# An encoder's first-layer values as seven quarter products ahead of the heads

## The chip, the cores and the metric

One core of a Trainium2 chip runs the whole program. The metric is the device time of one execution in microseconds (us): the median of 3 runs before the change is 657.52 us. Engines are named as the profile names them: PE (TensorE, with PEld for its weight loads), DVE (VectorE), ACT (ScalarE), POOL (GpSimd) and SP (SyncE, which issues most DMAs).

## The reference, cut to what matters

A two-layer encoder over 512 tokens of width 1024. Layer 0 mixes tokens by neighbourhood attention, layer 1 by multi-head latent attention; each mixer's output is gated by SiLU(z), projected and added, and a gated per-layer embedding follows. The change is in layer 0's input projection, in the third of its four parts:

```python
def mixer_na(xn, w_in, rpb, w_out):
    B, S, _ = xn.shape
    hd = NA_HEADS * NA_HEAD_DIM
    q, k, v, z = jnp.split(xn @ w_in, 4, axis=-1)
    shp = (B, S, NA_HEADS, NA_HEAD_DIM)
    o = neighbourhood_attention(q.reshape(shp), k.reshape(shp), v.reshape(shp), rpb)
    return (o.reshape(B, S, hd) * jax.nn.silu(z)) @ w_out
```

`v` is a 512 x 1024 matrix: 512 normalised tokens times 1024 x 1024 weights, used by 16 heads of 64 columns.

## The kernel before, in words

**Arithmetic.** Every float32 factor of a product is kept as two float32r tiles: `hi`, a rounded copy that ACT writes, and `lo`, the remainder `x - hi`, which DVE or POOL writes. A product is then three: hi x hi, lo x hi and hi x lo. So a block of 128 tokens, 512 output columns and a depth of 1024 costs 3 x 8 = 24 matmuls of 512 columns. `load_w` (L72) loads a weight tile of 128 x 1024 into `wraw`, has ACT write `whi` (L83) and POOL `wlo` (L84); there are three slots of each ("wp" pool), so a new tile waits for the matmuls of the third one before it.

**Order.** The program is written in one order, and a scheduler makes the order on each engine from it: of the instructions that are ready it takes the one that stands first in the program. `issue_after` pins an instruction behind another one.

**Stages around the change.** The first stage ("pre" pool, L971) loads the transposed input into `xs` (eight tiles of 128 x 512), computes the embedding product of layer 0 (`ple`, its outputs stored to DRAM at L480), the row norms, and the gates z for head pairs 0 and 1; then it scales `xs` in place to the normalised input (L1019, DVE) and splits it into `xT`, hi on ACT (L1020) and lo on DVE and POOL in turn (L1021). Gates z for pairs 2 to 4 follow (L1022, multiplied at L176).

Then `na_heads` (L224) runs. `values()` (L230) makes the first 512 columns of v: four blocks of tokens in four PSUM banks, the weights in four tiles `na_v0` of 256 rows by 512 columns (the names in the profile leave the number out: `na_v`), 96 matmuls at L238, and evacuates them into tiles `vt` by `v_split` (L215). The two other quarters of v are made inside the loop over head pairs, when `project(4)` and `project(6)` start (L247 to L260): each loads two tiles `na_v1` and runs 4 x 24 matmuls of 256 columns (through `mms`, L107). `project(j)` otherwise makes the queries and keys of head pair j (48 matmuls of 512 columns), and `attend(j)` the two heads: scores (L351, L352), softmax, transposes (L386, L388), and the product with the values (L400). `project(j + 1)` stands ahead of `attend(j)` in the program. In `attend(0)` to `attend(7)` one sum for the seven-product gates is issued per head (`sum_step`, L518: POOL issues DMAs of 1 MB that add in DRAM).

**The seven-product form** is in the kernel already, for the gate of each layer (`gate_seven`, L567): a product of two 2 x 2 block matrices from seven block products instead of eight, with the sums of weight blocks made in DRAM by DMAs beforehand (`quarters`, `sum_step`), the mixes of the left factor made by DVE out of PSUM (`keep_half`), and the combining of results in PSUM banks. Its matmuls are at L643, and all its subtractions for weights run on POOL, in halves of 512 columns (L588).

Of the kernel before, what the change touches and what calls it, by code (L numbers as in the profile page):

```python
# [40 lines left out]
class Trunk:  # L41
# [182 lines left out]
    def na_heads(self, pool, xT, zs, oT):  # L224
        nc, a = self.nc, self.a
        xh, xl = xT
        X = lambda t, k, kt: t[k // 4][:, k % 4, kt * P:(kt + 1) * P]
        V, A, U = {}, {}, {}

        def values():  # L230

            pss = [self.psum(b) for b in ("T", "T", "T", "O")]
            for c in range(4):
                w = self.load_w(a["na_v0"][c], 1024)
                for i, (s, r) in enumerate(((0, 0), (1, 0), (0, 1))):
                    for kt, ps in enumerate(pss):
                        for k in (2 * c, 2 * c + 1):
                            nc.tensor.matmul(ps, X((xh, xl)[s], k, kt), w[r][:, k % 2 * S:(k % 2 + 1) * S],  # L238
                                             start=k == 0 and i == 0, stop=k == KD - 1 and i == 2)
            for g in range(2):  # L240
                V[g] = [pool.tile([P, S], F32R, name="vt", tag="vt", bufs=8) for kt in range(NT)]
            for kt, ps in enumerate(pss):
                for g in range(2):
                    self.v_split(V[g][kt], ps[:, g * 256:(g + 1) * 256])

        def project(j):
            if j in (4, 6):  # L247
                g = j // 2
                wv = [self.load_w(a["na_v1"][g - 2, c], 1024) for c in range(2)]
                vts = V[g] = []  # L250
                for kt in range(4):
                    ps = self.psum("mm")
                    W = lambda s, k: wv[k // 4][s][:, (k % 4) * 256:(k % 4 + 1) * 256]
                    t = [(X(xh, k, kt), W(0, k)) for k in range(KD)]
                    t += [(X(xl, k, kt), W(0, k)) for k in range(KD)]
                    t += [(X(xh, k, kt), W(1, k)) for k in range(KD)]
                    self.mms(ps[:, :256], t)
                    vt = pool.tile([P, S], F32R, name="vt", tag="vt", bufs=8)
                    self.v_split(vt, ps[:, :256])
                    vts.append(vt)  # L260
# [53 lines left out]
        values()  # L314
# [648 lines left out]
    def run(self):  # L963
# [7 lines left out]
        with tc.tile_pool(name="pre", bufs=4, reuse_waits="tile") as pool:  # L971
# [10 lines left out]
            xs = [pool.tile([P, S], F32, name="xT", tag="xT", bufs=8) for k in range(KD)]  # L982
# [18 lines left out]
            xt = [pool.tile([P, D], F32, name="x", tag="x", bufs=4) for t in range(NT)]  # L1001
# [5 lines left out]
            self.ple(pool, 0, "pe", 6, operands)  # L1007
# [15 lines left out]
        oT = ([self.bigtile(f"oh{g}") for g in range(2)], [self.bigtile(f"ol{g}") for g in range(2)])  # L1023
        with tc.tile_pool(name="na", bufs=2, reuse_waits="tile") as pool:
            last = self.na_heads(pool, xT, zs, oT)
# [143 lines left out]
def layouts(i):  # L1169
# [4 lines left out]
    f = {}  # L1174
# [9 lines left out]
    def tiles(w, n):  # L1184
        k, m = w.shape
        return w.reshape(k // P, P, m // n, n).transpose(2, 1, 0, 3)
# [4 lines left out]
    f["na_v1"] = c(tiles(w[:, 2560:3072], 256).reshape(2, P, 2, 1024).transpose(0, 2, 1, 3))  # L1191

    def rows(w):
        return c(tiles(w, S).reshape(2, P, 4, 1024).transpose(0, 2, 1, 3))

    f["na_v0"] = c(tiles(w[:, 2048:2560], S).reshape(P, 4, 1024).transpose(1, 0, 2))
# [63 lines left out]
```

## Time and profile before

| what | value |
| --- | --- |
| time, 3 runs | 657.03, 657.52 (median), 657.75 us |
| span of the profiled execution, first to last instruction | 655.8 us (its time outside the span isn't given) |
| mean granted PE clock in the span | 0.997 |
| PE busy | 646.2 us, 3419 matmuls |
| DVE, ACT, POOL busy | 398.1, 441.2, 433.8 us |
| read from and written to HBM | 89.99 and 25.17 MB |
| `values()` on PE | 44.92 to 66.68 us of the span |

How to read it: a row of the groups gives line, engine and operation, the tile written `<-` the tiles read, the shape and the count, then busy time and the mean of one in ns, then the engine's idle time ahead of them and what ended it. A row of a line's own view gives the shortest, median and longest duration in ns, and the first and last start. A row of the timeline gives start, length of a merged piece, engine and line. A row of the chain gives start, length, and what the end of the program was waiting on at that time. Durations of matmuls overlap, since they are pipelined; their pitch, from a piece of the chain divided by its count, is what they cost.

### The profile page before, as it was taken

The numbers are of one execution on the slowest core, as the hardware profiler recorded it, in microseconds if no ns is written. First come the engines' busy times: TensorE is split into PE (matmuls) and PEld (weight loads), VectorE is DVE, ScalarE is ACT, GpSimd is POOL, SyncE is SP. The second block draws the span as 40 slices with busy tenths as digits, with TensorE's granted clock in tenths as the row PEclk, the third lists the DMA queues.
The fourth block names the chain that finished last, engine by engine and source line by source line (L and its number), as shares of the span: only waits on it lengthen the run. The fifth ranks groups of instructions, "written<-read, shape, count | busy, mean of one in ns | idle before, by whom it ended". The sixth has DMA issues, their size and how long they took to land.

```text
span 655.8 us, 10132 instructions
## 1 busy us (share of the span) xinstructions
PE 646.2 (99%) x3419; PEld 551.6 (84%) x3419; DVE 398.1 (61%) x854; ACT 441.2 (67%) x879; POOL 433.8 (66%) x383
## 2 busy tenths in 40 slices
PE   9999999999999999999999999999999999999994
PEld 6888888998988888888899888888888888888884
DVE  6190355845646526569825613888888886464665
ACT  7672587766767743687743635897979897537855
POOL 0496475895685664697764626785969887436974
PEclk9999999999999999999999999999999999999998
DMA  9944254996675889435743334120111223673524
GB/s 329 348 134 140 96 197 134 249 233 143 215 161 184 199 171 373 169 129 157 252 120 114 103 98 148 51 76 5 64 55 65 65 71 123 226 287 129 191 67 160
DMA packets 44756, 102.18 MB, mean 156 GB/s; under 512 B 4640, under 2 KB 17696, under 8 KB 44704
## 3 DMA queue, kind: packets, MB, share of 16 engines
q1 hardware_dynamic: 33776, 83.97, 38.1%
q0 software_dynamic: 10496, 16.78, 11.8%
q10 hardware_dynamic: 432, 0.79, 0.3%
q8 instruction: 27, 0.44, 0.3%
q14 instruction: 25, 0.20, 0.1%
HBM read 89.99 MB, written 25.17 MB: 176 GB/s over the span
## 4 chain that ended last, share of the span: by engine, by line
PE 98%; ACT 0%; DVE 0%; issue 0%; POOLq 0%; POOL 0%
PE ps_mm L107 35%; PE ps_S L107 12%; PE ps_mm L751 7%; PE ps_T L139 6%; PE ps_T L643 5%; PE ps_O L863 5%; PE ps_mm L643 3%; PE ps_S L643 3%; PE ps_T L107 3%; PE ps_T L238 2%; PE ps_O L400 2%; PE ps_O L107 2%; PE ps_mm L701 2%; PE ps_mm L184 2%; PE ps_T L388 2%; PE ps_S L701 1%
## 5 line engine op out<-in xcount | busy, mean ns | idle before, releaser
L84 POOL TENSOR_TENSOR wwlo<-wraw,wwhi 128x1024 fp32r<-128x1024 f32 (+5 forms) x78 | 143.2, 1852 | 76.4 <-ACT wwhi L83 54.7
L83 ACT ACTIVATE wwhi<-wraw 128x1024 fp32r<-128x1024 f32 (+5 forms) x81 | 65.5, 832 | 61.1 <-issue 19.2
L588 POOL TENSOR_TENSOR wlo<-wraw,whi 128x512 fp32r<-128x512 f32 x56 | 73.6, 1346 | 25.2 <-ACT whi L586 19.0
L848 POOL TENSOR_TENSOR ex<-ex,rc 128x512 f32<-128x512 f32 x64 | 66.3, 1045 | 25.8 <-DVE rc L847 22.0
L846 ACT ACTIVATE ex<-ps_S,mx 128x512 f32<-128x512 f32 x64 | 44.0, 688 | 11.7 <-DVE mx L844 10.1
L844 DVE TENSOR_REDUCE mx<-ps_S 128x1 f32<-128x512 f32 x64 | 43.7, 682 | 8.3 <-PE ps_S L107 7.7
L96 DVE TENSOR_TENSOR pt_lo<-ps_T,pt_hi 128x512 fp32r<-128x512 f32 x64 | 43.1, 681 | 7.1 <-ACT pt_hi L94 6.7
L374 POOL TENSOR_TENSOR ex<-ex,rc 128x128 f32<-128x128 f32 (+1 forms) x64 | 36.1, 621 | 15.0 <-DVE rc L370 15.0
L107 PE MATMUL ps_mm<-xh,wwhi 128*128 128x512 f32 x152 | 40.3, 398 | 0.0
L94 ACT ACTIVATE pt_hi<-ps_T 128x512 fp32r<-128x512 f32 x64 | 37.8, 595 | 3.4 <-PE ps_T L139 3.0
L107 PE MATMUL ps_mm<-xl,wwhi 128*128 128x512 f32 x152 | 38.5, 391 | 0.0
L139 PE MATMUL ps_T<-ident,ex 128*128 128x128 f32 x256 | 38.3, 272 | 0.0
L107 PE MATMUL ps_mm<-xh,wwlo 128*128 128x512 f32 x152 | 38.2, 391 | 0.0
L139 PEld LDWEIGHTS ps_T<-ident,ex 128*128 128x128 f32 x256 | 31.5, 140 | 7.5
L107 PEld LDWEIGHTS ps_mm<-xh,wwlo 128*128 128x128 f32 x152 | 28.3, 188 | 6.0
L586 ACT ACTIVATE whi<-wraw 128x1024 fp32r<-128x1024 f32 x28 | 29.2, 1055 | 5.9 <-DMA wraw<-sum 3.0
L107 PEld LDWEIGHTS ps_mm<-xl,wwhi 128*128 128x128 f32 x152 | 28.3, 188 | 5.7
L205 DVE TENSOR_TENSOR u<-ps_O,u 64x512 f32<-64x512 f32 x32 | 22.0, 686 | 17.2 <-ACT u L204 16.7
L368 ACT ACTIVATE ex<-ex,mx 128x128 f32<-128x128 f32 (+1 forms) x64 | 30.3, 475 | 2.7 <-DVE mx L358 1.8
L107 PEld LDWEIGHTS ps_mm<-xh,wwhi 128*128 128x128 f32 x152 | 27.3, 188 | 4.8
L209 POOL TENSOR_TENSOR u<-u,z 128x512 f32<-128x512 f32 x16 | 21.9, 1371 | 13.6 <-DVE u L205 8.3
L107 PE MATMUL ps_S<-ko,qo 128*128 128x512 f32 x96 | 28.9, 409 | 0.0
(441 smaller groups left out, 1849.8 us busy)
## 6 DMA issues: line engine op xcount, KB each, us to landing
sum<-gate POOLq DMA_DIRECT2D x12, 1024.0 KB, 7.8
wraw<-na_qk SPq DMA_DIRECT2D x16, 512.0 KB, 3.4
wraw<-sum SPq DMA_DIRECT2D x16, 512.0 KB, 3.3
pe<-pe SPq DMA_DIRECT2D x31, 256.0 KB, 6.9
wraw<-gate SPq DMA_DIRECT2D x12, 512.0 KB, 3.3
wraw<-na_v SPq DMA_DIRECT2D x8, 512.0 KB, 4.1
sum<-sum POOLq DMA_DIRECT2D x4, 1024.0 KB, 10.9
wraw<-na_o SPq DMA_DIRECT2D x8, 512.0 KB, 5.4
```

The costliest lines, as they stand in the source:

```text
L83: nc.scalar.activation(hi[:, c], raw[:, c], AF.Copy)
L84: f = lambda e, c=c: e.tensor_tensor(out=lo[:, c], in0=raw[:, c], in1=hi[:, c].bitcast(F32), op=ALU.subtract)
L94: self.last_copy = nc.scalar.activation(hi, src, AF.Copy, scale=scale)
L96: nc.vector.tensor_tensor(out=lo, in0=src, in1=hi.bitcast(F32), op=ALU.subtract)
L107: last = self.last_mm = nc.tensor.matmul(out, l, r, start=i == 0, stop=i == n - 1)
L139: self.last_mm = self.nc.tensor.transpose(t[:, i * P:(i + 1) * P], b, self.ident)
L588: nc.gpsimd.tensor_tensor(out=lo[:, o], in0=raw[:, o], in1=hi[:, o].bitcast(F32), op=ALU.subtract)
L643: mm = nc.tensor.matmul(ps, l, r, start=j == 0 and p in banks, stop=j == 11 and p in (2, 3, 4), skip_group_check=True)
L751: self.last_mm = nc.tensor.matmul(PS[key], *terms[i], start=i == 0, stop=i == len(terms) - 1)
L844: nc.vector.reduce_max(mx, sp, axis=AX.X, negate=True)
L846: nc.scalar.activation(ex, sp, AF.Exp, bias=mx, accum_out=sm)
L848: nc.gpsimd.tensor_tensor(out=ex, in0=ex, in1=rc.to_broadcast([P, S]), op=ALU.mult)
```

## The change

- The values of all 16 heads are made ahead of the loop over heads, by a new function `values_seven`; `values()` and the value parts of `project(4)` and `project(6)` are gone. Tokens are halved, the depth is halved and the columns are halved; the seven products have 256 tokens (two blocks i of 128), a depth of 512 and 512 columns. Each takes 12 matmuls of 512 columns per block i. They run in the order 1, 2, 7, 6, 4, 5, 3, each matmul pinned behind the one before it.
- The mixes of x for products 7, 5, 6 and 3 are made by POOL in place in `xs` (now two tiles `xk` of four), each 128 x 1024; ACT writes their hi part and DVE their lo part, into four of the big tiles `V7`, `V5`, `V6`, `V3`, which take the slots of `raw`, the unscaled x of the z gates.
- The weights come as eight tiles of 128 x 1024 (`R`), loaded at the start of the stage's own pool. Four products use sums or differences of two quarters: DVE makes these in place, one tile of 1024 columns after another. ACT writes the hi part of each of the 14 tiles; DVE writes the lo part of the first tile of each product, POOL that of the second, in halves of 512 columns. The tiles are in the three slots of the "wp" pool and two pairs of their own ("vw").
- Results are combined in PSUM: product 2 is accumulated on 1, 4 on 7, 5 and 3 on 6, with copies by ACT and sums by DVE between; `v_split` evacuates into `Q`, four tiles of 128 x 4 x 512, of which heads read slices.
- The first stage's pool is laid out anew (an unused tile `pad`, eight tiles for the embedding's outputs in place of six), so that the new pool's tiles come to lie on tiles that are free early. POOL's space for DMA descriptors goes to 8192, half of the default.

The parts that do the work, from the diff:

```diff
+    def values_seven(self, pool, xT, X, Q):
+        R = {p: [pool.tile([P, 1024], F32, name=f"v{p}{c}", bufs=1) for c in range(2)] for p in (1, 2, 3, 5)}
...
+        home = {7: (5, 5, 3, ALU.add), 6: (5, 5, 1, ALU.add), 4: (2, 2, 5, ALU.add), 5: (1, 5, 3, ALU.subtract)}
+        order = (1, 2, 7, 6, 4, 5, 3)
...
+        def prep(p):
+            nonlocal pieces
+            W[p] = []
+            for c in range(2):
+                raw = R[p][c] if p not in home else None
+                if raw is None:
+                    d, x, y, op = home[p]
+                    raw = R[d][c]
+                    nc.vector.tensor_tensor(out=raw, in0=R[x][c], in1=R[y][c], op=op)
+                own = pieces < 5 or pieces % 5 < 3
+                pieces += 1
+                hi, lo = ((self.wp if own else pool).tile([P, 1024], F32R, name=t, tag=t if own else "vw", bufs=3 if own else 4)
+                          for t in ("whi", "wlo"))
+                nc.scalar.activation(hi, raw, AF.Copy)
+                for o in (slice(0, S), slice(S, 2 * S)):
+                    (nc.gpsimd if c else nc.vector).tensor_tensor(out=lo[:, o], in0=raw[:, o], in1=hi[:, o].bitcast(F32),
+                                                                  op=ALU.subtract)
+                W[p].append((hi, lo))
...
+        banks = {1: "mm", 7: "S", 6: "T"}
+        base = {2: 1, 4: 7, 5: 6, 3: 6}
...
+        for p in order[:2]:
+            prep(p)
+        mm = self.last_mm
+        for n, p in enumerate(order):
+            if n + 2 < len(order):
+                prep(order[n + 2])
+            for i in range(2):
...
+                m = [(left(p, s, k, i), W[p][k // 2][r][:, k % 2 * S:(k % 2 + 1) * S])
+                     for c in range(2) for s, r in ((0, 0), (1, 0), (0, 1)) for k in (2 * c, 2 * c + 1)]
+                for j, (l, r) in enumerate(m):
+                    with self.tc.issue_after(mm.ins):
+                        mm = nc.tensor.matmul(ps, l, r, start=j == 0 and p in banks, stop=j == 11 and p in (2, 3, 4),
+                                              skip_group_check=True)
...
         def project(j):
-            if j in (4, 6):
-                g = j // 2
-                wv = [self.load_w(a["na_v1"][g - 2, c], 1024) for c in range(2)]
...
-        values()
         last = project(0)
...
+            for p, d, y, op in ((7, (0, lo), (0, hi), ALU.subtract), (5, (0, hi), (1, hi), ALU.subtract),
+                                (6, (1, hi), (0, lo), ALU.add), (3, (1, lo), (1, hi), ALU.subtract)):
+                d, y = (xk[g][:, :, c] for g, c in (d, y))
+                nc.gpsimd.tensor_tensor(out=d, in0=d, in1=y, op=op)
+                t = XV[p] = self.bigtile(f"V{p}")
+                h, l = (t[:, 2 * s:2 * s + 2, :].rearrange("p a (b c) -> p (a b) c", b=2) for s in range(2))
+                nc.scalar.activation(h, d, AF.Copy)
+                nc.vector.tensor_tensor(out=l, in0=d, in1=h.bitcast(F32), op=ALU.subtract)
```

More of the change, by code (lines that the diff above doesn't have):

```diff
@@ L261, in project, with na_heads @@
+    def na_heads(self, pool, xT, zs, oT, Q):
+        nc, a = self.nc, self.a
+        A, U = {}, {}
+        V = [[Q[kt // 2, g // 2][:, kt % 2 * 2 + g % 2, :] for kt in range(NT)] for g in range(4)]
+        def project(j):
             wq = self.load_w(a["na_qk"][j], 1024)
@@ L1190, in layouts @@
     f["na_z"] = c(tiles(w[:, 3072:], P).reshape(8, P, 1024))
-    f["na_v1"] = c(tiles(w[:, 2560:3072], 256).reshape(2, P, 2, 1024).transpose(0, 2, 1, 3))
     def rows(w):
         return c(tiles(w, S).reshape(2, P, 4, 1024).transpose(0, 2, 1, 3))
-    f["na_v0"] = c(tiles(w[:, 2048:2560], S).reshape(P, 4, 1024).transpose(1, 0, 2))
+    f["na_v"] = rows(w[:, 2048:3072])
     f["na_o"] = rows(i["na_w_out"][0])
```

94 lines of the change are left out of this document (58 added, 36 removed).

## The prediction

> **What bounds the kernel now.** I read the page's busy shares and its chain first, then the chain piece by piece, a table of busy time by stage, and last, for the stretch in which the change works, the timelines of DVE and GpSimd (POOL). From the page:
>
> ```profile
> PE 646.2 (99%) x3419; PEld 551.6 (84%) x3419; DVE 398.1 (61%) x854; ACT 441.2 (67%) x879; POOL 433.8 (66%) x383
> ...
> PE 98%; ACT 0%; DVE 0%; issue 0%; POOLq 0%; POOL 0%
> ```
>
> The chain that ends last is TensorE alone. So the kernel is the length of its matmul stream, and a change pays if it shortens the stream without opening gaps in it. The table by stage shows where the value products stand:
>
> ```profile
> core 0: us, PE busy (x) PEld busy (x) DVE busy (x) ACT busy (x) POOL busy (x), PEclk, DMA share, GB/s
> ...
> 28.12:44.92 16.80, 16.80 (x78) 13.91 (x77) 11.84 (x15) 12.82 (x19) 13.71 (x7) 1.00 0.62 221
> 44.92:66.68 21.76, 21.76 (x97) 18.02 (x97) 3.72 (x4) 5.66 (x7) 14.24 (x10) 1.00 0.39 125
> 66.68:119.00 52.32, 52.32 (x268) 44.31 (x268) 28.50 (x85) 36.59 (x78) 33.08 (x30) 1.00 0.48 142
> ```
>
> 44.92 to 66.68 is the first half of the values; in it DVE is busy for 3.72 us and ACT for 5.66, which is the room that the change uses. POOL has only 7.5 us free there. In 66.68 to 119, where heads run and no value product does, PE is still busy throughout: heads stay bound by PE when nothing of the values fills them.
>
> **PE's side: what is saved.** The pieces of the chain that give one matmul's pitch:
>
> ```profile
> 39.48 5.44 PE ps_mm L107 x24
> 44.92 1.36 PE ps_T L238 x6
> ...
> 131.13 1.78 PE ps_mm L107 x15
> ...
> 299.44 16.32 PE ps_T L643 x72
> ```
>
> A product of 512 columns takes 1.36/6 = 0.2267 us, in the seven-product code of the gate (L643, 16.32/72) just as here. One of 256 columns takes 1.78/15 = 0.119. How many of the latter there are:
>
> ```profile
> L107 PE MATMUL ps_mm<-wwhi,xl 128*128 128x256 f32 x64 | 10.1, 287 | 0.0
> L107 PE MATMUL ps_mm<-wwlo,xh 128*128 128x256 f32 x64 | 10.1, 289 | 0.0
> L107 PE MATMUL ps_mm<-wwhi,xh 128*128 128x256 f32 x64 | 9.5, 287 | 0.0
> ```
>
> Removed: 96 of 512 columns (21.76 us, the stage) and 192 of 256 (192 x 0.119 = 22.8 us, inside the heads), 44.6 in all. Added: 7 x 2 x 12 = 168 of 512, 38.1 us. PE saves 6.5 us. The new stage would run from 44.92 to 83.0 in an unbroken stream, 5.44 us for each of the seven products (24 matmuls). The heads lose their 22.8 us in full, by the 66.68 row above; the two weight loads in them go too, with four subtractions on POOL.
>
> **The other engines' side: what the new stage must get done.** Per product, two weight tiles of 1024 columns are split: a copy on ACT, and a subtraction of both halves, on DVE for the first tile and on POOL for the second. Four products need their two weight tiles summed first, on DVE (1024 columns each); four mixes of x run on POOL and their remainders on DVE (1024 each). What one costs alone, and what becomes of it when both engines work:
>
> ```profile
> L445 DVE TENSOR_TENSOR wlo<-wraw,whi x6: 684/686/693, 4.9 to 8.2; 128x512 fp32r<-128x512 f32 x6
> L84 DVE TENSOR_TENSOR wwlo<-wraw,wwhi x3: 691/1222/1226, 228.3 to 562.0; 128x1024 fp32r<-128x1024 f32 x2, 128x512 fp32r<-128x512 f32 x1
> L96 DVE TENSOR_TENSOR pt_lo<-ps_T,pt_hi x64: 669/680/693, 414.8 to 561.1; 128x512 fp32r<-128x512 f32 x64
> L586 ACT ACTIVATE whi<-wraw x28: 1042/1052/1067, 264.1 to 632.1; 128x1024 fp32r<-128x1024 f32 x28
> ...
> L94 ACT ACTIVATE pt_hi<-ps_T 128x512 fp32r<-128x512 f32 x64 | 37.8, 595 | 3.4 <-PE ps_T L139 3.0
> ```
> ```profile
> 31.08 7.15 POOL L84 TENSOR_TENSOR wwlo<-wraw,wwhi 128x1024 fp32r<-128x1024 f32 x3 [4.11 <-ACT wwhi L83]
> ...
> 268.51 7.56 POOL L588 TENSOR_TENSOR wlo<-wraw,whi 128x512 fp32r<-128x512 f32 x6 [0.72 <-ACT whi L586]
> ...
> 39.56 0.68 DVE L176 TENSOR_TENSOR z<-ps_S,R 128x512 f32<-128x512 f32 x1
> 40.15 4.12 DVE L1021 TENSOR_TENSOR xl<-xT,xh 128x512 fp32r<-128x512 f32 x2
> ...
> 41.97 5.16 POOL L1021 TENSOR_TENSOR xl<-xT,xh 128x512 fp32r<-128x512 f32 x3
> ...
> 249.23 2.74 POOL L84 TENSOR_TENSOR ww<-wraw,ww 128x1024 fp32r<-128x1024 f32 x1 [0.60 <-ACT ww L83]
> ...
> 250.13 2.92 DVE L84 TENSOR_TENSOR ww<-wraw,ww 128x1024 fp32r<-128x1024 f32 x1 [0.42 <-ACT ww L83]
> ```
>
> Alone, POOL takes 7.15/3 = 2.38 us for 1024 columns and 7.56/6 = 1.26 for 512. When DVE subtracts SBUF tiles at the same time, they take turns: two DVE subtractions of 512 last 4.12 us, not 1.4, and POOL's three take 5.16/3 = 1.72 each, so each DVE one adds 0.46. For 1024 columns, DVE's ends at 253.05, which is 1.08 after POOL's end at 251.97. DVE's operations with one operand in PSUM (the 64 at L96: 669 to 693 ns, next to a busy POOL) don't take part in this.
>
> So I count DVE's and POOL's work on SBUF tiles as one queue. It starts at 39.56, when DVE is through with scaling x, with POOL still holding three splits of x and DVE four. POOL: 3 x 1.26 + 14 halves x 1.26 + 4 mixes x 2.38 = 30.9 us. DVE: (4 splits of x + 14 halves) x 0.46 + (8 weight sums + 4 remainders of mixed x) x 1.08 = 21.3 us. Sum 52.2, so the last half of the last product's weights is ready at 91.8. In an unbroken stream it would be used by the eleventh pitch of product 3, at 44.92 + 6 x 5.44 + 11 x 0.2267 = 80.05. PE would be 11.7 us late.
>
> The same count to the earlier products (in the order 1, 2, 7, 6, 4, 5, 3): product 7 needs 21.6 us of the queue (to 61.2, due 58.3: 2.9 late), product 6 another 11.5 (72.7, due 63.7: 9.0), product 4 another 5.6 (9.1 late), product 5 another 6.7 (10.4), product 3 the last 6.9. Lateness is the largest of these, not their sum. The first remainder, on DVE, is queued behind the splits of x, which already run to 47.7 there, while product 1 wants it at 45.8: some 3 us, within the 11.7.
>
> The bounds of this term: if the two engines didn't hinder each other, DVE alone would need 18 x 0.69 + 12 x 1.22 + 17 x 0.68 (with a PSUM operand, before the last product: three gates z, eight sums of banks, six evacuations) = 38.6 us from 39.56, to 78.2, before 80.05, so 0 late. If each DVE subtraction cost its whole solo duration on top of POOL's, DVE's part would be 18 x 0.69 + 12 x 1.22 = 27.1 in place of 21.3, and 17.5 late. I take 11.7, since the two rows in which the engines meet, 5.16 and 2.92, are the case itself. A rule of the Trainium skill speaks against this change too: "SBUF — State Buffer", section "Who interferes with whom", says that a VectorE instruction with two SBUF inputs and a GpSimd instruction that reads SBUF exclude each other for the whole of an instruction. By that rule as written the queue is the longer one, 17.5 late; the turns in this trace agree with it in kind, and cost less, 0.46 for 0.69.
>
> **What I cost at nothing.** ACT: 18 copies of 1024 columns at 1.05 and 14 of 512 at 0.6, 27.3 us of the stage. Copies and sums of PSUM banks between products: the bank is used next after the other half's 12 matmuls, 2.72 us, against about 1.4 for copy and sum; without that cover, 1.4 each. The loads:
>
> ```profile
> sum<-gate POOLq DMA_DIRECT2D x12, 1024.0 KB, 7.8
> ...
> pe<-pe SPq DMA_DIRECT2D x31, 256.0 KB, 6.9
> ...
> wraw<-na_v SPq DMA_DIRECT2D x8, 512.0 KB, 4.1
> ```
> ```profile
> 24.05 3.02 SPq L480 DMA_DIRECT2D pe<-pe  x2
> 33.51 5.08 SPq L82 DMA_DIRECT2D wraw<-na_v  x3
> ```
>
> It is as many loads as before, now all ahead of the heads on SP's queue. Behind them stand the loads of the first head's weights, which aren't needed before 83; a load is 4.1 us, and no more than that would show if the cover failed. They wait for tiles of the first stage; the last of these, a store of the layer's embedding, is issued by 27.1 and lands 6.9 later, at 34, about when SP issues three of the value loads now. POOL issues the 16 sums in DRAM with half the descriptor space; its issue costs nothing on the chain now, and the bound is a wait of one landing, 7.8, inside heads with slack; I take 0.
>
> **The sum.** The profiled execution has a span of 655.8 us; the median of the runs is 657.52, 1.7 above it, and I keep that 1.7. 655.8 - 6.5 + 11.7 = 661.0 for the span, **662.7** for the time. A difference under 0.2% (1.3 us) can't be told from none.
>
> **Rivals.** (1) Faster: the gaps are filled. The order of instructions on each engine is made by a scheduler that puts ready matmuls where PE is free, as the chain shows where heads and projections mix:
>
> ```profile
> 97.11 0.46 PE ps_mm L107 x2
> 97.58 0.11 PE ps_T L386
> 97.68 0.23 PE ps_mm L107
> 97.92 0.10 PE ps_O L400
> ```
>
> The query and key products of the first head pair depend on nothing in the new stage but its weight slots and banks; they are 48 matmuls, 10.9 us. If it puts them between products, or runs the queue's work where nothing else stands, the lateness is hidden: 651.0 with all of it, 655.7 with 7 us of it. Against: the seven products are chained to each other and hold both "mm" banks until product 2 is out, and a scheduler that doesn't know of the turns sees no gap to fill. It decides when under 6.5 us of lateness is left. Chance 0.30. (2) Slower still: a single gap is long enough that PE's clock drops. At the start the matmuls of 512 columns come at 4.85/11 = 0.44 us:
>
> ```profile
> 0.76 4.85 PE ps_T L975 x11
> ```
>
> If a gap brings that back for as long, it costs 4.85 x (1 - 0.2267/0.44) = 2.4 us; twice, 667.5. Before has no such gap, so nothing of it can be seen there. Chance 0.12. "TensorE: Matmul & The Clock Gate" of the Trainium skill, section "What's actually happening", has the clock halve after about 3.4 us of idling; no run here shows it yet. (3) The products are saved, and heads give the time back, because their POOL work now has less PE time to hide behind: then the 22.8 isn't earned in full. The 66.68 row, 33.08 of POOL in 52.32, speaks against it. At a loss of 3 us it would be 665.7; chance 0.08.
>
> **How the numbers follow.** The forecast, lateness between 8 and 17.5, 659.0 to 668.5, has 0.50; 0.08 of that lies by its upper end, where a turn costs DVE's whole solo duration. Rival 1 gives 0.27 to faster and 0.03 to no change; the forecast's low edge gives 0.06 to no change, and 0.44 to slower; rival 2's 0.12 and rival 3's 0.08 are slower but for 0.05, of which 0.03 faster, 0.02 same, if PE saves more than I count. Faster 0.30, same 0.11, slower 0.59. The range goes from 652.0, leaving out the best of rival 1, to 668.5, the bound of the queue: within it the forecast's own is 659.0 to 668.5.
>
> **What would show it.** PE busy falls by 6.5 us and shows idle time for the first time, nearly all in the new stage, which lasts about 50 us for its 168 matmuls; what ends the idle time is a remainder written by DVE or POOL. In it, DVE's subtractions of 512 SBUF columns take 1.1 us and more and POOL's 1.7. After it heads are as dense as before, without 256-column products. I am wrong if matmuls of the query and key projections stand between the seven products, if the gaps end with ACT or a DMA, or if DVE's subtractions take 0.69 there.

## The result, and the profile after

The kernel takes **675.09 us** (median of 4 runs, 673.86 to 676.46) where before takes 657.49 beside it: a ratio of 1.027, 95% interval 1.0255 to 1.0284. It is slower, as forecast, but by 17.6 us and not by 5. The span of its profiled execution is 671.8 us, against 661.0 in the sum.

From the page of after, busy time by engine and the chain that ended last:

```profile
PE 644.6 (96%) x3299; PEld 543.7 (81%) x3299; DVE 436.5 (65%) x880; ACT 453.0 (67%) x887; POOL 448.4 (67%) x393
...
PE 90%; POOL 3%; DVE 2%; ACT 2%; issue 1%; DMA 1%; POOLq 0%; ACTq 0%; DVEq 0%
```

PE has 120 matmuls fewer, but its busy time falls by 1.6 us and not by 6.5, and its share of the chain falls from 98% to 90%. The table by stage of after shows where (span, then busy time and count of each engine, granted clock, DMA share, GB/s):

```profile
core 0: us, PE busy (x) PEld busy (x) DVE busy (x) ACT busy (x) POOL busy (x), PEclk, DMA share, GB/s
28.00:44.50 16.50, 16.46 (x75) 13.32 (x73) 10.16 (x16) 10.37 (x16) 12.15 (x6) 1.00 0.67 248
44.50:57.98 13.48, 0.00 (x1) 0.00 (x1) 10.52 (x5) 5.86 (x7) 11.15 (x5) 0.64 0.43 173
57.98:67.00 9.02, 9.02 (x31) 7.25 (x32) 6.69 (x7) 4.87 (x6) 5.32 (x4) 0.78 0.01 2
67.00:94.33 27.33, 23.53 (x91) 17.55 (x90) 24.28 (x23) 13.22 (x17) 15.53 (x10) 0.94 0.00 0
94.33:108.39 14.06, 14.06 (x64) 11.65 (x63) 5.37 (x8) 5.46 (x7) 7.23 (x5) 1.00 0.33 111
108.39:160.00 51.61, 51.61 (x271) 43.97 (x271) 30.22 (x88) 37.25 (x78) 36.96 (x35) 1.00 0.55 162
```

PE does nothing at all for the 13.5 us ahead of product 1; behind this gap the granted clock is low (0.78) and 31 matmuls last 9.02 us, 0.29 each where 0.2267 was counted; in the 27 us behind that, 3.8 us are idle. From 94.33 to 160 PE is busy throughout, and no wait of PE is listed behind that. What PE waited for, in the view of waits of after:

```profile
PE ps_mm L283 <- ACT whi L251: 13.5, 1, 13.5
PE ps_T L283 <- POOL wlo L253: 1.9, 2, 1.7
PE ps_S L283 <- DVE ps_S L268: 0.8, 2, 0.4
PE ps_T L283 <- ACT whi L251: 0.6, 1, 0.6
PE ps_S L283 <- POOL wlo L253: 0.5, 1, 0.5
```

**An account that closes.** Without any lateness the span would be 655.8 - 6.5 = 649.3 us, and PE's busy time 646.2 - 6.5 = 639.7. After is 22.5 above the first: 17.3 us of waits (the five rows) and 644.6 - 639.7 = 4.9 us more busy time for the same matmuls. Together 22.2. Most of the 4.9 is the halved clock: PE is busy for 7.0 us in steps in which the record of the clock has it halved, and a matmul there takes 0.427 us in place of 0.2267, so 7.0 x (1 - 0.2267/0.427) = 3.3 us. The rest lies at full clock, at the matmuls next to a wait: the last one before a wait and the first one behind it last 0.1 to 0.3 us longer in the trace. This split is used for every kernel below.

**Why the first gap is so long.** The timelines of ACT and POOL in after (start, length, engine, line; in brackets the idle time ahead and what ended it):

```profile
46.94 1.06 ACT L1087 ACTIVATE V<-xT 128x1024 fp32r<-128x1024 f32 x1 [1.08 <-POOL xT L1084]
49.36 1.06 ACT L1087 ACTIVATE V<-xT 128x1024 fp32r<-128x1024 f32 x1 [1.37 <-POOL xT L1084]
52.64 1.06 ACT L1087 ACTIVATE V<-xT 128x1024 fp32r<-128x1024 f32 x1 [2.22 <-POOL xT L1084]
55.92 1.06 ACT L1087 ACTIVATE V<-xT 128x1024 fp32r<-128x1024 f32 x1 [2.22 <-POOL xT L1084]
56.88 2.94 ACT L251 ACTIVATE whi<-v 128x1024 fp32r<-128x1024 f32 x3
...
44.53 11.36 POOL L1084 TENSOR_TENSOR xT<-xT 128x1024 f32<-128x1024 f32 x4
58.95 3.31 POOL L253 TENSOR_TENSOR wlo<-v,whi 128x512 fp32r<-128x512 f32 x2 [3.06 <-ACT whi L251]
```

On ACT the four copies of the mixed x (V) stand ahead of every copy of a weight tile. Each waits for its mix on POOL, and POOL needs 11.36 us for the four. So the first weight tile of product 1, which needs no mix at all, is copied only at 56.88. The groups of the stage in after (busy time, mean ns of one, idle time ahead and what ended it):

```profile
L253 POOL TENSOR_TENSOR wlo<-v,whi 128x512 fp32r<-128x512 f32 x14 | 22.7, 1647 | 17.6 <-ACT whi L251 17.5
L253 DVE TENSOR_TENSOR wlo<-v,whi 128x512 fp32r<-128x512 f32 x14 | 13.5, 1007 | 3.0 <-ACT whi L251 3.0
L246 DVE TENSOR_TENSOR v<-v,v 128x1024 f32<-128x1024 f32 x8 | 13.5, 1713 | 0.0
L1084 POOL TENSOR_TENSOR xT<-xT 128x1024 f32<-128x1024 f32 x4 | 11.1, 2781 | 0.2
L1088 DVE TENSOR_TENSOR V<-xT,V 128x1024 fp32r<-128x1024 f32 x4 | 10.1, 2521 | 3.0 <-ACT V L1087 2.8
```

The turns on SBUF are there (DVE's sums take 1.71 us in the mean against 1.21 alone, its V remainders 2.52), but POOL also stands idle for 17.5 us, waiting for ACT. ACT's copies wait in their turn: 5.8 us of the stage for weight sums by DVE, behind the first gap.

### The profile page after: what moved, and what is told of

The parts are those of the page before. It is cut to its first block, busy times and chain, and to the rows that moved or that the text cites. A ratio compares the mean times of both kernels' runs of the same rounds, so it can differ in the third digit from the quotient of the medians.

```text
span 671.8 us, 9959 instructions
## 1 busy us (share of the span) xinstructions
PE 644.6 (96%) x3299; PEld 543.7 (81%) x3299; DVE 436.5 (65%) x880; ACT 453.0 (67%) x887; POOL 448.4 (67%) x393
## 4 chain that ended last, share of the span: by engine, by line
PE 90%; POOL 3%; DVE 2%; ACT 2%; issue 1%; DMA 1%; POOLq 0%; ACTq 0%; DVEq 0%
PE ps_mm L107 30%; PE ps_S L107 11%; PE ps_mm L804 6%; PE ps_T L139 6%; PE ps_T L696 5%; PE ps_O L916 4%; PE ps_mm L696 3%; PE ps_S L696 3%; PE ps_T L107 2%; PE ps_T L283 2%; PE ps_O L453 2%; PE ps_O L107 2%; PE ps_mm L754 2%; POOL xT L1084 2%; PE ps_mm L184 2%; PE ps_T L441 2%
## 5 line engine op out<-in xcount | busy, mean ns | idle before, releaser
L84 POOL TENSOR_TENSOR wwlo<-wraw,wwhi 128x1024 fp32r<-128x1024 f32 (+5 forms) x70 | 123.7, 1779 | 59.0 <-ACT wwhi L83 46.8
L83 ACT ACTIVATE wwhi<-wraw 128x1024 fp32r<-128x1024 f32 (+5 forms) x73 | 57.2, 807 | 40.3 <-PE ps_mm L107 14.3
L899 ACT ACTIVATE ex<-ps_S,mx 128x512 f32<-128x512 f32 x64 | 44.0, 687 | 12.1 <-DVE mx L897 10.5
L427 POOL TENSOR_TENSOR ex<-ex,rc 128x128 f32<-128x128 f32 (+1 forms) x64 | 36.5, 640 | 14.3 <-DVE rc L423 13.5
L107 PE MATMUL ps_mm<-xh,wwhi 128*128 128x512 f32 x152 | 42.1, 403 | 0.0
L107 PE MATMUL ps_mm<-xl,wwhi 128*128 128x512 f32 x152 | 40.0, 396 | 0.0
L107 PE MATMUL ps_mm<-xh,wwlo 128*128 128x512 f32 x152 | 39.3, 393 | 0.0
L253 POOL TENSOR_TENSOR wlo<-v,whi 128x512 fp32r<-128x512 f32 x14 | 22.7, 1647 | 17.6 <-ACT whi L251 17.5
L209 POOL TENSOR_TENSOR u<-u,z 128x512 f32<-128x512 f32 x16 | 21.5, 1345 | 16.2 <-DVE u L205 10.4
L205 DVE TENSOR_TENSOR u<-ps_O,u 64x512 f32<-64x512 f32 x32 | 21.9, 684 | 12.7 <-ACT u L204 12.3
```

Source lines behind the costliest of these rows:

```text
L83: nc.scalar.activation(hi[:, c], raw[:, c], AF.Copy)
L84: f = lambda e, c=c: e.tensor_tensor(out=lo[:, c], in0=raw[:, c], in1=hi[:, c].bitcast(F32), op=ALU.subtract)
L107: last = self.last_mm = nc.tensor.matmul(out, l, r, start=i == 0, stop=i == n - 1)
L899: nc.scalar.activation(ex, sp, AF.Exp, bias=mx, accum_out=sm)
```

## The experiments

Two theories at the start. **A**: ACT's order is the cause, with the V copies ahead of the weight copies. **B**: the amount of DVE's and POOL's work sets the end, in whatever order it is done. A third, **C**, was late loads: SP issues the value loads at 37 to 43 us, later than I had put them. All kernels, each timed beside before (657.3 to 657.5 in every group); "waits" is the sum of PE's rows in the view of waits from 28 us on, "longer busy" PE's busy time above 639.7, and "halved" the part of it that the halved steps explain, as worked out above:

| kernel | median us | ratio, 95% interval | waits | longer busy | halved |
| --- | --- | --- | --- | --- | --- |
| after | 675.09 | 1.0255 to 1.0284 | 17.3 | 4.9 | 3.3 |
| e1_loads: loads first | 675.65 | 1.0244 to 1.0288 | 17.5 | 7.2 | 5.1 |
| e2_nomix: no mixes of x | 665.99 | 1.0120 to 1.0150 | 8.7 | 6.3 | 4.5 |
| e3_wfirst: weights ahead of the mixes | 675.36 | 1.0259 to 1.0290 | 15.9 | 7.9 | 5.8 |
| e4_warm: dummy matmuls in the gap | 676.30 | 1.0277 to 1.0308 | 7.1 | 16.9, dummies in it | 2.5 |
| e7_mixdve: mixes on DVE | 671.69 | 1.0196 to 1.0230 | 14.1 | 5.6 | 4.7 |
| e8_prodonly: one weight prepared | 655.45 | 0.9962 to 0.9983 | 2.8 | 1.5 | 1.5 |
| e9_nosums: no weight sums | 670.79 | 1.0192 to 1.0226 | 15.7 | 3.5 | 2.8 |
| e10_nlate2: one gate product ahead | 671.52 | 1.0201 to 1.0232 | 14.3 | 5.9 | 4.2 |
| f1_nl1: two gate products ahead | 676.52 | 1.0271 to 1.0301 | 17.2 | 8.1 | 5.9 |
| f2_nl1_mix: two, mixes on DVE | 675.07 | 1.0249 to 1.0280 | 14.6 | 9.8 | 6.8 |
| f3_nl0_mix: three, mixes on DVE | 676.26 | 1.0271 to 1.0301 | 14.6 | 10.3 | 6.3 |
| b_nl1: before, two gate products ahead | 665.16 | 1.0098 to 1.0132 | 5.2 | 2.7 over before | 2.2 |
| g1_wfirst_mix: weights first, mixes on DVE | 674.08 | 1.0237 to 1.0268 | 12.8 | 10.1 | 8.4 |
| g2_mix_nl2: one gate product, mixes on DVE | 670.49 | 1.0177 to 1.0211 | 12.7 | 7.1 | 5.7 |
| g3_wfirst_mix_nl2: all three | 673.70 | 1.0233 to 1.0264 | 16.7 | 6.9 | 3.4 |
| g4_nox: weights prepared, x unmixed | 662.96 | 1.0068 to 1.0098 | 7.5 | 4.3 | 3.2 |
| h5_byneed: order of need | 672.52 | 1.0215 to 1.0246 | 12.3 | 8.9 | 6.4 |
| h8_byneed_nl2: the same, one gate product | 671.83 | 1.0195 to 1.0229 | 13.3 | 8.1 | 5.6 |

In every row but e4's, waits and longer busy time together are the span above 649.3 (above 655.8 in b_nl1) to within 0.5 us, so the view of waits lists nearly all that PE stood idle for. What halved steps don't explain comes to 0.2 to 0.4 us for each wait in every row but e8's: by this count, many short waits cost more than one long one of the same length.

### What the preparation costs, piece by piece

**e8_prodonly**, the products alone (`left`, which picks the tiles of x, then takes unmixed tiles of `xT`):

```diff
+            if p != 1:
+                W[p] = W[1]
+                return
...
-            for p, d, y, op in ((7, (0, lo), (0, hi), ALU.subtract), (5, (0, hi), (1, hi), ALU.subtract),
+            for p, d, y, op in () and ((7, (0, lo), (0, hi), ALU.subtract), (5, (0, hi), (1, hi), ALU.subtract),
```

> All seven products use the weights of the first and the unmixed x: no mix of x, no V copy, no weight sum, and one preparation of two weight tiles in place of seven; the loads, the 168 matmuls and the evacuations stay (the output is another one). If PE's saving is 6.5 us and heads earn all of theirs: 657.3 less 6.5, plus a start of 1 to 3 us late for the first weights: 651 to 654. If heads give time back (my third rival), over 655.

655.45, 4.6 above 650.9. The view of waits and the table by stage of e8:

```profile
PE ps_mm L284 <- ACT whi L254: 2.8, 1, 2.8
```
```profile
44.40:47.35 2.95, 0.16 (x2) 0.01 (x1) 1.31 (x4) 2.23 (x4) 0.00 (x0) 0.97 1.02 407
47.35:50.60 3.25, 3.25 (x8) 2.58 (x9) 1.27 (x2) 1.84 (x2) 2.28 (x2) 0.50 0.78 311
50.60:54.00 3.40, 3.40 (x17) 2.81 (x16) 0.00 (x0) 0.60 (x1) 3.30 (x4) 1.00 0.02 5
```

Its PE is never late again after the start. The 8 matmuls of the row at half the clock would take 1.81 us at full clock and took 3.25, so 1.4 us were lost there: 653.7 - 2.8 - 1.4 = 649.5, which is 6.3 us under before, of the 6.5 that I counted; heads give next to nothing back. But even a wait of 2.8 us is followed by 3.25 us at a clock of 0.50, with 8 matmuls where the next 3.40 us hold 17: its time passes my mark of 655 by the late start and the halved clock, and not by the heads. The first weight copy comes at 46.26, behind the last gate's z on ACT; I had product 1 start at 44.92.

**g4_nox** prepares all seven weights, and leaves x unmixed (the edit of the loop above alone, with `left` taking tiles of `xT`):

> All seven weights are prepared as in after, but x stays unmixed in all products: no mix, and no V copy or V remainder (the output is another one). It stands between the kernel without any preparation but the first (655.5) and the one without the mixes alone (666.0). If weight sums and splits fit beside the products and only x's tiles hold them up: 655 to 657. If the weights' queue on DVE and GpSimd sets the end by itself, as my sum had it (29 of the 52 us, turns counted): over 660.

662.96: over 660, so the preparation of the weights makes PE late by itself, with x out of it. **e2_nomix** has the V copies and remainders too, and lacks only the mixes:

```diff
                 d, y = (xk[g][:, :, c] for g, c in (d, y))
-                nc.gpsimd.tensor_tensor(out=d, in0=d, in1=y, op=op)
```

> POOL's four mixes of x are left out (products 7, 5, 6 and 3 use unmixed quarters of x, so the output is another one); the copies and remainders of those quarters stay. Theory A: ACT's four copies wait for nothing on POOL any more; the gap falls from 13.5 to about 5 us (four copies of 1.05 and one weight copy), time 664 to 667. Theory B (DVE and POOL taking turns sets the stage's length): only POOL's 11.1 us of mixes leave the queue, which gaps later in the stage, 5 us in all, show; the first gap stays over 10 us and the time over 669.

665.99: as A expected. The gap ahead of product 1 falls from 13.5 to 5.1:

```profile
PE ps_mm L283 <- ACT whi L251: 5.1, 1, 5.1
PE ps_T L283 <- POOL wlo L253: 2.3, 2, 1.7
```

So there is a ladder from 650.9 to 675.1: 4.6 us for a late start, 7.5 for the weights' sums and splits, 3.0 for the copies and remainders of the mixed x, 9.1 for the mixes on POOL. **e9_nosums** takes the other end first:

```diff
                     raw = R[d][c]
-                    nc.vector.tensor_tensor(out=raw, in0=R[x][c], in1=R[y][c], op=op)
```

> DVE's eight sums of weight quarters are left out, and the first operand's quarter is used as it is (the output is another one). That takes 8 x 1.1 to 1.2 us from DVE, and as much from the queue that it forms with GpSimd. Theory A: the first gap of 13.7 us and the cold matmuls after it stay; of the later gaps (5 us, with 1.4 us of a second cold stretch) most go: 669 to 672. Theory B (the queue's total sets the end): 675 less about 9, 665 to 667. If the later gaps are ACT's, 674 to 676.

670.79, with the first gap still 13.5: in A's range. B's number, 9 us less, fails as it stands: the eight sums are worth 4.3 us when all else is there.

### Loads, clock, order

**e1_loads** pins the first loads of query and key weights behind the value loads on SP:

```diff
-                nc.sync.dma_start(R[p][c], self.a["na_v"][n, c0 + c])
+                self.last_v = nc.sync.dma_start(R[p][c], self.a["na_v"][n, c0 + c])
...
+            with self.tc.issue_after(self.last_v.ins):
                 wq = self.load_w(a["na_qk"][j], 1024)
```

> The loads of the value weights are issued ahead of the first three query and key weight loads; nothing else is changed. Theory A (order on ACT: the first weight copies stand behind the four copies of mixed x, which wait for POOL's mixes): the 13.5 us gap before the first product stays within 1 us, time 673 to 676. Rival C (late loads: SP issues the value loads at 37 to 43 us, behind query and key loads that wait for slots): the gap shrinks by 5 us or more, time under 670.

675.65, no change: the gap is 12.1 us, 1.4 less than in after, and still ends with ACT's copy. C falls for after; the loads could be left at nothing there.

**e4_warm** keeps PE busy in the gap with matmuls of ones into a free bank:

```diff
         mm = self.last_mm
+        for i in range(60):
+            with self.tc.issue_after(mm.ins):
+                mm = nc.tensor.matmul(dummy, *ones, start=True, stop=True)
```

> 60 matmuls of ones (13.6 us) are put on PE ahead of the first product, into a bank that is free then; their result is used nowhere. They fill the gap and do nothing for the order. If the halved clock costs what its pitch says (ten matmuls at 0.427 in place of 0.227 us and a first one at 0.59, 2.3 us), the time falls by 2 to 2.5 us, to 672.5 to 673; if the clock comes back by itself within the wait, nothing changes; the second halving, at 82 us, stays.

676.30, a miss. The matmuls behind the gap ran at full clock (a granted clock of 1.00 from 57.9 to 68 us), and had to wait there instead: PE stood idle for 2.2 us of these 10.1, and from 57.98 to 67 in after for none. The waits of e4:

```profile
PE ps_S L288 <- DVE ps_S L268: 3.7, 1, 3.7
PE ps_mm L288 <- DVE wlo L253: 2.2, 2, 1.2
PE ps_T L288 <- POOL wlo L253: 1.2, 1, 1.2
```

So in this run matmuls at half the clock and waits stood in for each other: the time that PE gained at the start was lost where the next tile was not ready.

**e3_wfirst** splits the weights of product 1 and the first tile of product 2 ahead of the mixes (three tiles are loaded a second time, into the slots of "wp"):

```diff
+            for c in range(3):
+                raw, h, l = (self.wp.tile([P, 1024], d, name=n, tag=n, bufs=3)
+                             for n, d in (("wraw", F32), ("whi", F32R), ("wlo", F32R)))
+                nc.sync.dma_start(raw, a["na_v"][0, c])
+                nc.scalar.activation(h, raw, AF.Copy)
...
+                early.append((h, l))
             lo, hi = slice(0, 2 * P), slice(2 * P, S)
```

> Three of the four weight tiles of products 1 and 2 are loaded and split ahead of the mixes in the program, through the usual three slots; all work of the changed kernel is still done, and 1.5 MB more is loaded. Theory A: product 1 starts when the gates end, the first gap is under 2 us, PE's clock isn't halved there (2.3 us), and of the 22.5 us of lateness what the turns cost is left, 8 to 12: time 660 to 665. Theory B: the queue of DVE and POOL is as long as before, so gaps move into the later products and the time stays over 668.

675.36: A's number is missed, and B's came: the gap moved. The waits of e3:

```profile
PE ps_mm L287 <- ACT whi L255: 8.4, 1, 8.4
PE ps_mm L287 <- DVE z L176: 2.6, 1, 2.6
```

PE now starts product 1 at 44.16, waits 2.6 us in the middle of it, and 8.4 ahead of the fourth weight tile, whose copy is still behind the four V copies. A is therefore true of the first gap, and no account of the time. But this run doesn't test the order alone. The three early loads take the slots of "wp", so that loads of query and key weights wait for slots, and the value loads behind them on SP are issued at 54.4 to 58 us and not at 37 to 43. The fourth tile's copy waits 2.3 us for its load at the end of the 8.4, and DVE's first sum 3.9 us for another. So C comes back here, and in g1 and g3 below, which have the same edit (2.1 and 5.4 us ahead of that copy); e1's order of loads was not joined with it.

**e7_mixdve** moves the mixes to DVE (`nc.gpsimd` to `nc.vector` at L1084):

> The four mixes of x run on DVE in place of GpSimd. Theory A (ACT's queue holds the V copies, which wait for the mixes, ahead of the weight copies): DVE needs about 1.2 us a mix where GpSimd needed 2.35 to 3.2, but starts them only behind its splits of x, near 47.5; the last mix ends near 53 instead of 55.9, the first weight copy starts 2 to 4 us earlier, and the gap before product 1 (13.5 us in after) falls to 9 to 11. Time 670 to 673. Theory B (one queue of DVE's and GpSimd's work sets the end, in whatever order): 5 us less of it, time near 670, with the first gap as long as before and the later ones gone. If neither matters (the value loads set the start), 675.

671.69: both theories' time. The first gap of 9.2 us is what A expected, and not B's, and 4.9 us of later waits are left. **g1_wfirst_mix** joins this with e3's edit:

> The first three weight tiles split ahead of the mixes, and the mixes on DVE. Theory A1 (two things hold PE up by about the same length, the weight copies' place on ACT behind the mixes, and the mixes' own length on GpSimd; taking away one leaves the other): both gone, the gap before product 1 is 3 us or less, the one before the fourth tile 3 to 4 instead of 8.4, with one halved clock fewer: 667 to 670. Theory A2 (the order is worth nothing; DVE's, GpSimd's and ACT's work for seven products takes that long in any order): 671 to 673, as with the mixes on DVE alone.

674.08, worse than e7 alone; neither A1 nor A2 has it. Its waits are shorter than e7's (12.8 for 14.1), but lie in six places instead of three, and the halved steps cost it 8.4 us for 4.7. Part of the waits is the late loads.

**h5_byneed** does all the work of after in the order of need: e3's early weights; the mixes (for 7 and 6 on POOL, for 5 and 3 on DVE) written to free `wraw` tiles instead of in place; and the split of the mixed x for 6, 5 and 3 only when its product is prepared:

```diff
+            for e, p, x, y, op in ((nc.gpsimd, 7, (0, lo), (0, hi), ALU.subtract), (nc.gpsimd, 6, (1, hi), 7, ALU.add),
+                                   (nc.vector, 5, (0, hi), (1, hi), ALU.subtract), (nc.vector, 3, (1, lo), 6, ALU.subtract)):
+                if p == 3:
+                    self.split_x(XV[7], RAW[7])
...
             if n + 2 < len(order):
+                if order[n + 2] in (6, 5, 3):
+                    self.split_x(X[order[n + 2]], RAW[order[n + 2]], behind.ins)
                 prep(order[n + 2])
```

> The same work, in the order in which the products need it: product 1's weights and the first tile of product 2 are split ahead of the mixes; the mixes (two on GpSimd, two on DVE) are written to free weight tiles; the splits of the mixed x for products 6, 5 and 3 are pinned on ACT behind the weights of the product before. Theory D (DVE and GpSimd as one queue have the size that I summed, and it was wrong to take it in the order of need): served by need, the lateness is near the 11.7 us of the sum, and 2 to 4 us of halved clock come on top: 661 to 667. Theory E (the queue isn't the bound, but ACT's copies that wait for DVE and GpSimd in turn, whatever the order): 671 to 675, as in all orders so far.

672.52: E's time. No value load is waited for here. Page, waits and a part of the table by stage of h5:

```profile
PE 648.6 (97%) x3299; PEld 545.6 (81%) x3299; DVE 442.1 (66%) x882; ACT 453.2 (68%) x887; POOL 445.8 (66%) x391
```
```profile
PE ps_mm L295 <- POOL wlo L263: 2.6, 2, 1.7
PE ps_mm L295 <- DVE z L176: 2.6, 1, 2.6
PE ps_S L295 <- DVE ps_S L278: 2.5, 1, 2.5
PE ps_T L295 <- POOL wlo L263: 2.3, 2, 1.7
PE ps_S L295 <- POOL wlo L263: 2.1, 2, 1.7
PE ps_mm L295 <- DVE wlo L1098: 0.2, 1, 0.2
```
```profile
49.90:57.10 7.20, 6.01 (x23) 4.14 (x23) 7.17 (x4) 3.61 (x5) 6.23 (x4) 1.00 0.04 17
57.10:68.60 11.50, 7.69 (x25) 5.56 (x24) 11.38 (x10) 5.18 (x6) 6.26 (x3) 0.85 0.03 3
68.60:78.90 10.30, 7.94 (x24) 5.52 (x24) 10.30 (x12) 5.16 (x7) 3.90 (x2) 0.83 0.13 47
78.90:86.20 7.30, 4.84 (x13) 3.49 (x13) 7.30 (x6) 4.91 (x6) 7.29 (x4) 0.77 0.00 0
```

There is no long gap any more, and the waits are 12.3 us in all, near the 11.7 of the sum. This nearness is in part luck: 7.2 us of them end with a remainder, as I forecast, but 2.6 end with DVE's multiplication for a gate z, and 2.5 with DVE's sum of a PSUM bank, which my sum puts at nothing. They lie in nine pieces, the clock is halved four times, and PE's busy time grows by 8.9 us where D allowed 2 to 4; the halved steps explain 6.4 of it. By e4, a full clock would not give all of that back: part of it would turn into waits. How much was not measured.

The table shows what limits h5: DVE is busy for 36.15 of the 36.3 us from 49.9 to 86.2, and POOL for 23.7. No wait of PE ends with ACT, but E is not refuted by that: from 46 to 97, POOL's remainders wait 18.8 us for ACT's copies, and these 8.5 us for DVE's sums. Work that would go from DVE to POOL in this order, such as a part of the sums or remainders, was not tried.

### Covering the gap with gate products

`NLATE` is the number of gate products z that are computed behind the heads; one fewer is one more product of 5.44 us ahead of the values (`NLATE = 3` to `2`, `1`, `0`; in f1 to f3 the copies `s1` move to the stage's own tiles).

> One of the three gate products of 24 matmuls that stand behind the heads is computed ahead of the values (5.44 us of PE, its load, two copies on ACT, its remainder on GpSimd or DVE). Theory A: PE has 5.4 us of work for the first gap, the copies and the remainder move the mixes by 1 to 3 us: the gap falls by 2.5 to 4.5, time 671 to 673, if the end of the heads needs no third gate product to fill it; if it does, up to 3 us are given back there. If the work that is moved ahead delays the mixes as much as it covers: 675.

671.52: the gap is 9.3 us, as expected.

> Two of the three late gate products are computed ahead of the values (10.9 us of PE), with product 1's two copies s1 kept in tiles of the value stage. Theory A: each gate product covers about 4 of the first gap net of its own preparation, as one took it from 13.7 to 9.5 us; the gap is 5 to 6 us, and the time falls by as much again as with one: 667 to 669. If what PE gains there is only handed on to later waits (everything after the gap is as late as before, since DVE, GpSimd and ACT are the bound): 671 to 672.

676.52: the first gap fell to 7.7 only, and the end of the heads lost more than was gained. The control shows why:

> Control: the kernel before with two of its late gate products computed ahead of the values. Before has no gap there, so that the move has nothing to cover: the time stays within 1 us of 657.4, or rises by up to 3 where the end of the heads then has gaps. If it falls by over 1.3, the gain of the moved gate products is not the cover of the new stage.

665.16: 7.8 us slower, outside what I expected. The longest of its waits:

```profile
PE ps_mm L107 <- ACT ww L83: 4.4, 1, 4.4
```

The late gate products cover a wait of 4.4 us behind the heads, for a weight of the output projection; with two of them moved it is bare, and the clock halves behind it. Less those 7.8 us f1 would stand at 668.7, in A's range; this is an estimate, and A's gap of 5 to 6 us is missed all the same.

> Two gate products ahead of the values, and the mixes of x on DVE. Theory A: the mixes alone took the first gap from 13.7 to 9.4 us, two gate products take 8 more: 1 to 2 us are left of it, with a halved clock of no more than 1.7 us behind it; the later gaps (4.1 and 1.7 us with the mixes on DVE, and a second halving of 2.4) stay: 662 to 665. If covers add up to no more than the larger of the two (a common later bound on DVE's and GpSimd's work): 668.

675.07, or 667.3 without the same 7.8: near the second theory's 668, and not A's 662 to 665; the first gap is still 4.7 us. The covers hardly add.

> All three late gate products ahead of the values, and the mixes of x on DVE. Theory A: no first gap is left, and PE stands 3 us later at the later products than with two, so that their waits shrink too: 657 to 661. The bound below is PE's own saving: before less 6.5, 651. If the end of the heads has nothing to fill it without the gate products, up to 3 us are given back.

676.26: no gain from the third; the first gap is 3.0 us, the later waits are as they were, and 4.4 us are lost at the end as in f1.

> The mixes of x on DVE, and one late gate product ahead of the values. If the two gains (3.4 and 3.6 us) add: 667 to 669. With two gate products the end of the heads gave back 7.8 us (a wait of 4.4 us there for a copy of a later weight); with one, 1.4 of that wait was left, so that little is given back. If they don't add: 671.

670.49, the best of the versions that do the whole work, and still 13 us above before: the two gains of 3.4 and 3.6 make 4.6, so they don't add.

> All three: weight tiles split first, mixes on DVE, one late gate product ahead of the values. Theory A1: no gap before product 1 (3 us less the 4 that a gate product covers net), and about 3 before the fourth tile, under the length that halves the clock: 662 to 665. Theory A2: 667 to 669, as without the weights first.

673.70, in neither range: weights first costs 3.2 here, as it cost 2.4 in g1, and the late loads are part of this price (5.4 us ahead of the fourth tile's copy).

> The same, and one late gate product ahead of the values. Theory D: it covers 3 to 4 us of the lateness, and the end of the heads gives 1.4 to 2 back: 1 to 3 us below the kernel that is ordered by need alone, 659 to 665. Theory E: 670 to 674.

671.83: 0.7 below h5, and in E's range.

So no version with the whole work comes near before. Eleven kernels that do it in different orders and on different engines, after among them, with at most one gate product moved, lie between 670.5 and 676.3, while each piece of work that is left out brings 3 to 9 us: the preparation makes PE late, and the orders tried decide mostly where. Whether its amount alone is the bound, or its division between DVE and POOL and the way through ACT, stays open: DVE was full in h5, and POOL was not. Not tried: weight sums or remainders moved from DVE to POOL, the value loads ahead of others in e3, g1 and g3, a full clock in the order of need, and gap-free covers other than gate products.

## Why the prediction was wrong in size

- **PE's saving, 6.5 us**: right. In before, 589.1 us lie behind the value stage (66.68 to 655.8); in after 563.4 lie behind 108.39, and 14 of the first head's projection matmuls (3.17 us) stand ahead of it: 566.6. Heads gain 22.5 of the 22.8. e8 gives 6.3 of the 6.5.
- **Rival 1, gaps filled**: 14 matmuls stood between the last products, where PE wasn't waiting; none in the gaps. Rightly not forecast.
- **The queue, 52.2 us**: it took this long, but not as I counted it. From 39.56 us on, the time in which DVE or POOL works on one of these tiles is 52.3 us in after (the union of their pieces at L1077, L1084, L1088, L246 and L253), and it ends at 96.2, with 4.3 us in which neither does. My count has POOL at work all the time and DVE's operations put in between; in after POOL works for 38.8 of the 52.3 us, DVE for 39.3, and both at once for 25.7. That the two numbers meet is luck. DVE's work on PSUM, which I left out of the queue since it takes no turns, takes up DVE all the same: in h5, five such operations, 3.4 us, lie in the 36.15 in which DVE is full. "SBUF — State Buffer" of the Trainium skill, section "Who interferes with whom", has the two engines exclude each other: the rows agree, a DVE half takes 0.69 us alone and up to 1.78 beside POOL, while POOL's takes 1.29 alone and 2.29 beside a DVE sum.
- **"The same count to the earlier products"**: this is the step that failed. It let the queue serve the products in the order of need: product 7 at 61.2, product 6 at 72.7. In after the mixes and splits for the last two products come ahead of the first weight; product 7's last remainder ends at 73.97 and product 6's at 82.75, which is 15.7 and 19.0 us after they were due; the forecast had them 2.9 and 9.0 late. The largest lateness is that of product 6, in the middle; product 3's last remainder, at 96.21, is 16.2 late.
- **"The first remainder ... some 3 us, within the 11.7" and "ACT at nothing"**: wrong together. ACT's 27.3 us are no load, but its order ties DVE and POOL together: 13.5 us of wait ahead of product 1, and a part of the 17.5 us that POOL is idle (later copies wait for DVE's sums). h5, in the order of need and with two mixes on DVE, has 12.3 us of waits in place of 17.3, near the whole of what they exceed the forecast by, though its time is only 2.6 us shorter. Even there product 6's last remainder comes at 78.86 and not at 72.7: POOL stands idle from 68.6 to 75.0 ahead of it, for a tile that DVE, busy all that time, must sum and ACT copy first. That chain within a tile isn't in my count; I read it from the trace and didn't try it by itself.
- **Rival 2, the halved clock**: it didn't take the place of the forecast, it came on top. The sum has it at nothing; halved steps cost 3.3 us in after and 1.5 to 8.4 in the other kernels, and stopping and starting at each wait another 1.6 in after. I gave it 0.12 and asked for one long gap. It takes far less (below).
- **The sum of the miss** in the span, 671.8 for 661.0: 5.6 us more of waits and 4.9 of longer busy time. The profiled run took 673.86 us, so 2.1 us lie outside its span where I put 1.7; the other 1.2 is that this run lies below the median. In before, too, 1.8 to 2.1 us lie outside the span of one and the same run: I had set the span of one run against the median of three.
- **My signs of being wrong**: they came. Of the waits of after, 14.1 us end with ACT; 14 matmuls of the first head's projection stand between the last products; and DVE's subtractions of 512 columns take 0.69 us in the median, with a mean of 1.01 from the few beside POOL's.
- **Loads at nothing**: right (e1). **Rival 3**: didn't occur.

## What to carry to other kernels

Count what an idle-looking engine must do before the *first* use, in the order in which every queue will really do it: an instruction that is ready can stand behind one that waits for another engine. Where a change trades PE time for preparation, price the preparation by leaving it out piece by piece; if the time falls with each piece and hardly with the order, look for the engine that is full in the best order before trying another one. And PE that waits often pays twice: short waits slow the matmuls behind them.

## What the runs showed of the hardware

The granted clock goes in steps of 3.41 us, and what counts is how much of a step PE is idle, not one long pause. Two answers of the table by stage, for such steps of after and of e9:

```profile
79.02:82.43 3.41, 1.70 (x5) 0.86 (x5) 3.41 (x4) 2.36 (x4) 3.19 (x2) 1.00 0.00 0
82.43:85.85 3.42, 3.05 (x7) 2.48 (x8) 3.42 (x4) 1.65 (x4) 3.38 (x3) 0.50 0.00 0
```
```profile
77.60:81.00 3.40, 2.31 (x11) 1.55 (x9) 2.70 (x3) 1.69 (x3) 2.96 (x2) 1.00 0.00 0
81.00:84.40 3.40, 3.39 (x15) 2.78 (x16) 1.20 (x2) 2.05 (x3) 0.66 (x1) 1.00 0.00 0
```

In the first, PE is idle for 1.71 of 3.41 us, and the next step is at half the clock; in the second, a step of e9, it is idle for 1.09, and the next step is at full clock. With the steps laid out from each trace's clock record, over the traces of this study from 28 to 300 us, of 42 steps at full clock with PE idle for 1.71 us or more, 41 were followed by a halved one; of 28 with 0.8 to 1.7, one was. In e10 one such step had three pauses of at most 0.64 us each, 1.72 in all, and the next step was halved. In a halved step a 512-column matmul takes 0.427 us instead of 0.2267. "TensorE: Matmul & The Clock Gate" of the Trainium skill, section "What's actually happening", has the halving after about 3.4 us of idling; the step agrees, the idle time that suffices is about half of it here.
